# Strassen weights in a ring of their own, a fourth lo buffer, and the negated copy ahead of the hi cast, in a two-layer decoder trunk

## The chip, the cores and the metric

The kernel runs on one core of a Trainium2 chip. The metric is the device time of one execution in microseconds (us). Engines are TensorE (PE in the profile, its weight loads PEld), VectorE (DVE), ScalarE (ACT), GpSimd (POOL) and SyncE (SP, which here only issues DMAs). POOL issues a second, small kind of DMA. A change of about 0.2% is the least that a measurement of this kernel can tell.

## The reference

`x` is 256 tokens by 2048 channels; all arrays are fp32. Cut to what matters here:

```
mem_n = rms_norm(mem, mem_norm_g)
for l in range(2):
    hn = rms_norm(x, mix_norm_g[l])
    x = x + (even_mixer if l == 0 else odd_mixer)(hn, ...)   # matmuls with 2048-wide weights, attention or short conv
    x = x + cross_attention(rms_norm(x, xattn_norm_g[l]), mem_n, xq[l], xk[l], xv[l], xo[l])
    x = x + sq_relu_mlp(rms_norm(x, mlp_norm_g[l]), mlp_w1[l], mlp_w2[l])
return rms_norm(x, final_norm_g)

def sq_relu_mlp(h, w1, w2):                                  # 2048 -> 8192 -> 2048
    return square(relu(h @ w1)) @ w2
```

## The kernel before, in words

**Numbers in two parts.** Every weight and every activation is split into a hi part (a cast to the matmul's reduced fp32 type) and a lo part (the value minus hi). A product is hi weights times both parts of the activation (one 512-wide matmul per 128 × 128 block of weights) plus lo weights times hi activation (256 wide).

**Weights.** `weights()` brings 512 KB, half of a 2048 × 128 chunk, into a `raw` tile by a DMA that SP issues (L159). ACT casts it into `whi` (L160), DVE subtracts into `wlo` (L165). `raw` has a ring of 5 buffers, `whi` and `wlo` rings of 3 each; a tile that is to be written waits until the readers of the tile that held its buffer are done. With `added`, lo is made without DVE: ACT writes the negated raw into `wlo` (L162), and a DMA issued by POOL adds raw to the rounded negative in place (L163, the accumulate DMA).

**A chunk.** `proj_long` takes the two halves of a chunk and issues 15 hi matmuls, 16 lo matmuls (8 of each half), and the last hi matmul, which closes the sum.

**The MLP.** `mlp` works in four quarters of 2048 hidden channels per layer. In each quarter 16 chunks of w1 give the hidden activation: ACT and DVE add the two halves of the result (`sum`, L211, L212), DVE applies relu and the norm's factor (L833), ACT squares into `uu` (L835). After every fourth chunk `uu` is split into `hid` (L839, L840), and in the first three quarters DVE combines its token and channel halves (`combine`, L740 to L743) and splits that into `hs` (L745, L746).

In these three quarters of both layers, so six times, the product with w2 follows as eight Strassen steps (`for s in range(8)`). A step does half of its channels with seven products instead of eight: `seven_weights` loads two raw tiles of 512 KB (`raws`, L760, out of the ring of `raw`), makes `shi` and `slo` from the first (L767, L768; in the rings of `whi` and `wlo`), forms half-tile differences in place on DVE (L769, L771, L773, L774), splits the block b22 (L770, L772), and splits two tiles of combinations, t2 with t3 and then t1 with t4 (`tw`, ACT L776 and DVE L777). `seven_step` issues 21 matmuls into seven sums `p`, in the order b11, b21, t1, t4, b22, t3, t2. Then `proj_long` with `added` does an ordinary chunk of w2 (`mmn` in the profile), its second half by way of the accumulate DMA, and `residual` adds the result to `x` (L327). So a step uses three `wlo` buffers: `slo`, first half, second half. The weights of the first step are asked for after chunk 12 of the quarter's w1, those of the next ones at the head of each step; `seven_sum` (L798 to L803) ends the stretch.

**What sets the order.** The code only states what depends on what. A scheduler decides each engine's list from this, from the buffers that come free and from the order in the code; DVE's lo subtractions keep the code's order among themselves (`ordered`), and the matmuls do in stretches marked `strict`. Each engine then runs its own list in order.

Of the kernel before, what the change touches and what calls it, by code (L numbers as in the profile page):

```python
# [45 lines left out]
def trunk(ctx: ExitStack, tc: tile.TileContext, d):  # L46
    nc = tc.nc
    V, A, T, G = nc.vector, nc.scalar, nc.tensor, nc.gpsimd
# [1 line left out]
    const = ctx.enter_context(tc.tile_pool(name="const", bufs=1))  # L50
    xpool = ctx.enter_context(tc.tile_pool(name="xpool", bufs=1))
    half = ctx.enter_context(tc.tile_pool(name="half", bufs=13))
    wraw = ctx.enter_context(tc.tile_pool(name="wraw", bufs=5))
    wspl = ctx.enter_context(tc.tile_pool(name="wspl", bufs=3))
    tmp = ctx.enter_context(tc.tile_pool(name="tmp", bufs=2))
    small = ctx.enter_context(tc.tile_pool(name="small", bufs=4))
    pools = {}
    ps_mm = ctx.enter_context(tc.tile_pool(name="ps_mm", bufs=4, space=bass.MemoryType.PSUM))
    ps_at = ctx.enter_context(tc.tile_pool(name="ps_at", bufs=3, space=bass.MemoryType.PSUM))
    ps_nm = ctx.enter_context(tc.tile_pool(name="ps_nm", bufs=1, space=bass.MemoryType.PSUM))  # L60
# [5 lines left out]
    x = xpool.tile([P, NC, S], F32, name="x")  # L66
# [24 lines left out]
    def load_vec():  # L91
        nc.sync.dma_start(out=vec, in_=d["vec"][:, NG:])
        lv = vec[:, VEC["lam"] - NG:VEC["lam"] - NG + 256].rearrange("p (a b) -> p a b", a=4)
        lp = tmp.tile([P, S], F32, tag="t32", name="lp", bufs=7)[:, :128].rearrange("p (a b) -> p a b", a=2)
# [53 lines left out]
    def weights(src, added=False):  # L148

        run_later(rate[0], calls[0])  # L150
        run_stages(calls[0])
        calls[0] += 1
        raw = wraw.tile([P, 1024], F32, tag="raw", name="raw")
        hi = wspl.tile([P, 1024], F32R, tag="whi", name="whi")
        lo = wspl.tile([P, 1024], F32R, tag="wlo", name="wlo")
        n = 512 if calls[0] == 1 else 1024
        for i in range(0, 1024, n):
            o = slice(i, i + n)
            nc.sync.dma_start(out=raw[:, o], in_=src[:, o])  # L159
            A.copy(hi[:, o], raw[:, o])  # L160
            if added:
                A.activation(lo[:, o], raw[:, o], AF.Copy, scale=-1.0)  # L162
                G.dma_start(out=lo[:, o], in_=raw[:, o], accum_op=ALU.add)  # L163
            else:
                ordered(V.tensor_tensor(lo[:, o], raw[:, o], f(hi[:, o]), op=ALU.subtract), "lo")  # L165
        return hi, lo

# [104 lines left out]
    def spread(rows):  # L272
        ps = ps_nm.tile([P, 512], F32, tag="nm", name="nmb")[:, :S]
        for t in range(2):
            dg = tmp.tile([P, P], F32, tag="diag", name="diag")
            A.activation(dg, ident, AF.Copy, scale=rows[:, t:t + 1])
            mm(ps[:, t * P:(t + 1) * P], ones, dg, start=True, stop=True)
        return ps

    def rstd_rows(acc, n, pool=None, name="rrow"):  # L280

        v = small.tile([P, 2], F32, tag="rs_v", name="rs_v")
        V.tensor_scalar(v, mean_rows(acc, n), EPS, None, op0=ALU.add)
        return rsqrt(v, 2, pool, name)
# [12 lines left out]
        return y  # L297

    def to_sbuf(ps, pool=None, name="rb"):
        r = pool.tile([P, S], F32, tag=name, name=name) if pool else tmp.tile([P, S], F32, tag="rb", name=name, bufs=3)  # L300
        A.copy(r, ps)
        return r

# [3 lines left out]
    class SumSq:  # L307
# [4 lines left out]
        def add(self, src):  # L312
            if self.first:
                A.activation(self.acc, src, AF.Square)
                self.first = False
                return
            sq = tmp.tile([P, S], F32, tag="sq", name="sq")
            A.activation(sq, src, AF.Square)  # L318
            V.tensor_tensor(self.acc, self.acc, sq, op=ALU.add)  # L319

    def tmp32(name="t32"):
        return tmp.tile([P, S], F32, tag="t32", name=name, bufs=7)

    def residual(k, ps, nxt, ss, gname):

# [28 lines left out]
    def even_mixer():  # L354
        xa, ss = Act(NC, "xn"), SumSq()
# [30 lines left out]
        rc, r = rr["col"], rr["bc"]  # L386
# [62 lines left out]
        def heads_out(h, ahl):  # L449
            po = ps_at.tile([P, 512], F32, tag="at", name="po")[:, :S]  # L450
            hs = slice(h * P, (h + 1) * P)
            for kt in range(2):
                o = slice(kt * S, (kt + 1) * S)
                mm(po, vh[:, kt, hs], ahl[:, 0, o], start=kt == 0, stop=False)
                mm(po, vl[:, kt, hs], ahl[:, 0, o], start=False, stop=False)
                mm(po, vh[:, kt, hs], ahl[:, 1, o], start=False, stop=kt == 1)
            osq = tmp.tile([P, S], F32, tag="sq", name="osq")
# [297 lines left out]
    def seven_weights(src):  # L755


        raw = [wraw.tile([P, 4, 2, P], F32, tag="raw", name="raws") for _ in range(2)]
        for i, t in enumerate(raw):
            nc.sync.dma_start(out=t.rearrange("p c k f -> p c (k f)"),  # L760
                              in_=src[4 * i:4 * i + 4].rearrange("c p f -> p c f"))
# [5 lines left out]
        A.copy(sh, b1)  # L767
        V.tensor_tensor(sl, b1, f(sh), op=ALU.subtract)  # L768
# [4 lines left out]
        V.tensor_tensor(b2[:, 1], b2[:, 1], b1[:, 0], op=ALU.subtract)  # L773
        V.tensor_tensor(b1[:, 1], b2[:, 1], b1[:, 1], op=ALU.subtract)  # L774
        for t, b in ((t1, b1), (t2, b2)):
            A.copy(t[:, 0], b)  # L776
            V.tensor_tensor(t[:, 1], b, f(t[:, 0]), op=ALU.subtract)  # L777
# [45 lines left out]
    def mlp(l, xa, ss, gname):  # L823
        r = rstd(ss.acc, D)
        nxt = nss = None
        w1, w2 = d[f"w1{l}"], d[f"w2{l}"]
        uu = half.tile([P, 2, 2, 4, P], F32, tag="half", name="uu")
        for qd in range(4):
            hid = Act(NC, "hid")
            sa = SevenAct(hid) if qd < 3 else None  # L830
            for c in range(NC):
                u = summed(proj_long(w1[qd * NC + c], xa))
                V.scalar_tensor_tensor(u, u, 0.0, r, op0=ALU.max, op1=ALU.mult)  # L833
                v = uu[:, c // 4 % 2]
                A.activation(v[:, c % 4 // 2, c % 2 * 2:c % 2 * 2 + 2].rearrange("p h f -> p (h f)"), u, AF.Square)  # L835
                if c % 4 == 3:
                    t = hid.t[c // 4]
# [29 lines left out]
        return nxt, nss  # L867

    def scoped(name, fn, *a):
        with tc.tile_pool(name=name, bufs=4) as pools[name]:  # L870
            return fn(*a)

    def attentions(first):
        a = even_mixer() if first else odd_mixer(*state)
        return cross(0 if first else 1, *a)

    state = scoped("att", attentions, True)
    state = scoped("mlp", mlp, 0, *state, "mix1")
    state = scoped("att", attentions, False)
    _, ss = scoped("mlp", mlp, 1, *state, "final_norm_g")  # L880

    r = spread(rstd_rows(ss.acc, D))
    for g in range(8):
        o = slice(2 * g, 2 * g + 2)
        V.tensor_tensor(x[:, o], x[:, o], r.rearrange("p (a s) -> p a s", a=1).broadcast_to([P, 2, S]), op=ALU.mult)  # L885
        nc.sync.dma_start(out=d["yT"][:, o], in_=x[:, o])


# [58 lines left out]
```

## Time and profile before

| | before |
|---|---|
| median of 3 runs | 2995.7 us (2995.38 to 2997.54) |
| the profiled execution | 2999.52 us, of which the span is 2997.6 |
| mean granted clock of TensorE | 0.986 |
| busy: PE, DVE, ACT, POOL | 97%, 73%, 54%, 1% |
| instructions | 42425 |
| bytes moved by DMA | 565.16 MB, mean 189 GB/s |

In the profile a row of waits names the engine and line that waits, whom it waits for, the total in us, how often, and the longest. A row of the timeline has the start, the duration, the engine and line, the operation with out<-in, and in brackets the idle time of the engine just before it and what ended that. A row of groups has the total busy time and the mean in ns, then the idle time ahead of the group's instructions. A row of windows has a stretch and its length, the busy times (and instruction counts) of PE, PEld, DVE, ACT and POOL, the granted clock, the DMA engines' busy share and GB/s.

### The profile page before, as it was taken

What the parts mean: (1) busy time and instruction counts of PE and PEld (TensorE: products, weight loads), DVE (VectorE), ACT (ScalarE), POOL (GpSimd) and SP (SyncE); (2) the same over time, 40 slices, a digit from 0 to 9 for tenths busy, and PEclk for the clock granted to TensorE, in tenths of its full rate; (3) what the DMA queues carried; (4) which work ended last, traced back from release to release, by engine and by line L of the source; (5) the groups of instructions that cost most, each with busy time, mean ns of one, the idle gap of its engine ahead of it and who ended that gap; (6) DMA issues with size and microseconds to landing.
All of it is one profiled execution on the core that took longest, in us unless ns stands there. A gap on an engine that the chain in (4) does not pass through costs nothing. (4 is left out here: it accounts for less than half of the span.)

```text
span 2997.6 us, 42425 instructions
## 1 busy us (share of the span) xinstructions
PE 2902.7 (97%) x16072; PEld 2529.8 (84%) x16072; DVE 2201.0 (73%) x3414; ACT 1605.3 (54%) x2275; POOL 44.7 (1%) x68
## 2 busy tenths in 40 slices
PE   9999999999999899999999999999999999999998
PEld 7888888888878778888888888888888787887887
DVE  7899987766777777766677765477767767777665
ACT  6666455555554555545444444455555545555553
POOL 0000000000000000000000000000000000000000
PEclk9999999999999999999999999999999999999999
DMA  7464665445576675766556656654455766757664
GB/s 248 160 200 159 194 190 189 156 155 183 179 208 201 181 218 175 211 201 190 183 193 202 197 195 191 193 187 159 154 181 180 205 202 184 224 182 206 199 187 139
DMA packets 194171, 565.16 MB, mean 189 GB/s; under 512 B 17456, under 2 KB 66736, under 8 KB 193968
## 3 DMA queue, kind: packets, MB, share of 16 engines
q1 hardware_dynamic: 187056, 537.30, 55.8%
q0 software_dynamic: 6912, 25.17, 4.3%
q8 instruction: 126, 2.06, 0.3%
q14 instruction: 77, 0.63, 0.1%
HBM read 535.13 MB, written 2.10 MB: 179 GB/s over the span
## 5 line engine op out<-in xcount | busy, mean ns | idle before, releaser
L165 DVE TENSOR_TENSOR wlo<-raw,whi 128x1024 fp32r<-128x1024 f32 (+1 forms) x865 | 1056.7, 1222 | 471.0 <-PE mm L139 187.2
L160 ACT CAST whi<-raw 128x1024 fp32r<-128x1024 f32 (+1 forms) x913 | 958.4, 1050 | 590.1 <-PE mm L139 271.8
L139 PE MATMUL mm<-xn,whi 128*128 128x512 f32 x3840 | 945.7, 394 | 0.0
L139 PEld LDWEIGHTS mm<-xn,whi 128*128 128x128 f32 x3840 | 708.3, 190 | 135.2
L139 PEld LDWEIGHTS mm<-xn,wlo 128*128 128x128 f32 x3840 | 507.5, 194 | 49.3 <-DVE wlo L165 25.9
L139 PE MATMUL mm<-xn,wlo 128*128 128x256 f32 x3840 | 516.8, 285 | 23.4 <-DVE wlo L165 23.4
L211 ACT COPY sum<-mm 128x256 f32<-128x256 f32 x272 | 101.1, 372 | 580.2 <-PE mm L139 580.0
L212 DVE TENSOR_TENSOR sum<-mm,sum 128x256 f32<-128x256 f32 x272 | 115.1, 423 | 105.7 <-ACT sum L211 105.3
L139 PE MATMUL mmn<-hid,whi 128*128 128x512 f32 x768 | 191.9, 392 | 0.0
L139 PEld LDWEIGHTS mmn<-hid,whi 128*128 128x128 f32 x768 | 145.5, 189 | 28.0
L139 PE MATMUL mmn<-hid,wlo 128*128 128x256 f32 x768 | 111.7, 293 | 48.5 <-DMA wlo<-raw 48.4
L139 PEld LDWEIGHTS mmn<-hid,wlo 128*128 128x128 f32 x768 | 103.4, 196 | 58.8 <-DMA wlo<-raw 55.0
L777 DVE TENSOR_TENSOR tw<-raws,tw 128x1024 fp32r<-128x1024 f32 x96 | 114.7, 1221 | 34.6 <-ACT tw L776 34.6
L139 PE MATMUL mmr<-whi,mem 128*128 128x512 f32 x512 | 137.3, 390 | 0.0
L139 PE MATMUL mm<-mem,whi 128*128 128x512 f32 x512 | 126.3, 393 | 0.0
L139 PE MATMUL mm<-o,whi 128*128 128x512 f32 x512 | 124.7, 392 | 0.0
L139 PE MATMUL mm<-hid,whi 128*128 128x512 f32 x512 | 122.7, 391 | 0.0
L139 PE MATMUL p<-tw,hs 128*128 128x512 f32 x432 | 116.6, 394 | 3.2 <-DVE tw L777 3.0
L511 DVE SCALAR_TENSOR_TENSOR cv<-a,vec,cv 128x255 f32<-128x255 f32 (+14 forms) x240 | 111.8, 466 | 2.9
L139 PEld LDWEIGHTS mmr<-whi,mem 128*128 128x128 f32 x512 | 95.8, 188 | 19.6
L139 PEld LDWEIGHTS mm<-hid,whi 128*128 128x128 f32 x512 | 94.1, 188 | 18.6 <-DVE hid L840 0.5
L139 PEld LDWEIGHTS mm<-o,whi 128*128 128x128 f32 x512 | 93.7, 188 | 18.6 <-DVE o L254 0.9
(208 smaller groups left out, 3284.3 us busy)
## 6 DMA issues: line engine op xcount, KB each, us to landing
raw<-w SPq DMA_DIRECT2D x416, 512.0 KB, 4.2
raws<-w SPq DMA_DIRECT2D x96, 512.0 KB, 3.9
raw<-odd_in SPq DMA_DIRECT2D x96, 512.0 KB, 4.6
raw<-even_in SPq DMA_DIRECT2D x64, 512.0 KB, 4.2
raw<-xk SPq DMA_DIRECT2D x64, 512.0 KB, 3.6
raw<-xv SPq DMA_DIRECT2D x64, 512.0 KB, 3.6
raw<-xq SPq DMA_DIRECT2D x64, 512.0 KB, 4.0
raw<-xo SPq DMA_DIRECT2D x64, 512.0 KB, 3.8
```

Source lines behind the costliest of these rows:

```text
L139: i = T.matmul(*a, **k)
L160: A.copy(hi[:, o], raw[:, o])
L165: ordered(V.tensor_tensor(lo[:, o], raw[:, o], f(hi[:, o]), op=ALU.subtract), "lo")
L211: A.copy(t, ps[:, S:])
L212: V.tensor_tensor(t, ps[:, :S], t, op=ALU.add)
L511: ordered(V.scalar_tensor_tensor(cv[:, c, s:], a[:, c, :S - s], col("conv_a_w", i + j), cv[:, c, s:], op0=ALU.mult, op1=ALU.add), "lo")
L777: V.tensor_tensor(t[:, 1], b, f(t[:, 0]), op=ALU.subtract)
```

## The change

- `raws` leave the ring of `raw`, which has 4 buffers instead of 5, for a ring of 4 of their own in the MLP's pool. `uu` leaves its tile of the pool `half` and takes tiles of that ring, one per four chunks.
- `wlo` has 4 buffers instead of 3. The tile with t1 and t4 moves into the place that `uu` left in `half`.
- With `added`, the negated copy and the accumulate DMA stand ahead of the hi cast.
- The small tiles `t32`, `rb`, `sq` and `diag` get their buffer counts by stage: 7, 3, 2, 2 as before in the mixers and cross-attention, 3, 1, 1, 1 in the MLP. The final norm moves into the MLP's stage (`last`).

```diff
-    wraw = ctx.enter_context(tc.tile_pool(name="wraw", bufs=5))
+    wraw = ctx.enter_context(tc.tile_pool(name="wraw", bufs=4))
...
+    BUFS = {"att": {"t32": 7, "rb": 3, "sq": 2, "diag": 2}, "mlp": {"t32": 3, "rb": 1, "sq": 1, "diag": 1}}
+
+    def scratch(tag, name, shape=(P, S)):
+        return pools[pools["now"]].tile(list(shape), F32, tag=tag, name=name, bufs=BUFS[pools["now"]][tag])
...
-        lo = wspl.tile([P, 1024], F32R, tag="wlo", name="wlo")
+        lo = wspl.tile([P, 1024], F32R, tag="wlo", name="wlo", bufs=4)
...
             nc.sync.dma_start(out=raw[:, o], in_=src[:, o])
-            A.copy(hi[:, o], raw[:, o])
             if added:
                 A.activation(lo[:, o], raw[:, o], AF.Copy, scale=-1.0)
                 G.dma_start(out=lo[:, o], in_=raw[:, o], accum_op=ALU.add)
-            else:
+            A.copy(hi[:, o], raw[:, o])
+            if not added:
                 ordered(V.tensor_tensor(lo[:, o], raw[:, o], f(hi[:, o]), op=ALU.subtract), "lo")
...
-        raw = [wraw.tile([P, 4, 2, P], F32, tag="raw", name="raws") for _ in range(2)]
+        raw = [pools["mlp"].tile([P, 4, 2, P], F32, tag="raws", name="raws", bufs=4) for _ in range(2)]
...
-        sl = wspl.tile([P, 2, 4, P], F32R, tag="wlo", name="slo")
+        sl = wspl.tile([P, 2, 4, P], F32R, tag="wlo", name="slo", bufs=4)
...
-        t1, t2 = [pools["mlp"].tile([P, 2, 2, 4, P], F32R, tag=f"tw{i}", name="tw", bufs=1) for i in range(2)]
+        t1 = half.tile([P, 2, 2, 4, P], F32R, tag="half", name="tw")
+        t2 = pools["mlp"].tile([P, 2, 2, 4, P], F32R, name="tw", bufs=1)
...
-        uu = half.tile([P, 2, 2, 4, P], F32, tag="half", name="uu")
...
-                v = uu[:, c // 4 % 2]
+                if c % 4 == 0:
+                    v = pools["mlp"].tile([P, 2, 4, P], F32, tag="raws", name="uu", bufs=4)
...
     def scoped(name, fn, *a):
+        pools["now"] = name
```

In the changed kernel the lines are numbered a little higher: the sum is L215, the negated copy L165, the accumulate DMA L166, the hi cast L167, the lo subtraction L169, `hs` L749 and L750, `shi` L772, `tw` L781 and L782, the square L840. The lists differ in many rows, since the scheduler makes them anew; the number of instructions on each engine is the same but for waits. Three places follow. In the rows, "waits" names the engines and DMA queues whose signal the instruction needs.

**First place: ACT in chunks 11 to 14 of a quarter, where the first step's weights are prepared.** `sum` is a chunk's result, `whi` an ordinary hi cast, `shi`, `b` and `tw` belong to the Strassen weights. Before, from chunk 11's sum on:

```order
L211 COPY sum<-mm 128x256 [waits PE_49]
L767 CAST shi<-raws 128x1024 [waits DMAHW5_49,Activation_49]
L835 ACTIVATE uu<-sum 128x256 [waits DVE_49]
L839 CAST hid<-uu 128x4x256 [waits Activation_49]
L160 CAST whi<-raw 128x1024 [waits DMAHW7_49,PE_49]
L211 COPY sum<-mm 128x256 [waits PE_49]
L160 CAST whi<-raw 128x1024 [waits DMAHW0_49]
L776 CAST tw<-raws 128x1024 [waits DVE_49]
L745 CAST hs<-uu 128x8x128 [waits DVE_49]
L835 ACTIVATE uu<-sum 128x256
L776 CAST tw<-raws 128x1024 [waits DVE_49]
L160 CAST whi<-raw 128x1024 [waits DVE_49,DMAHW1_49,PE_49,Activation_49]
```

After, from chunk 12's sum on:

```order
L215 COPY sum<-mm 128x256 [waits PE_49]
L749 CAST hs<-uu 128x8x128 [waits DVE_49]
L840 ACTIVATE uu<-sum 128x256 [waits DVE_49]
L772 CAST shi<-raws 128x1024 [waits DMAHW1_49]
L167 CAST whi<-raw 128x1024 [waits DMAHW5_49]
L775 CAST b_8436<-raws 128x512 [waits DMAHW2_49]
L167 CAST whi<-raw 128x1024 [waits DMAHW6_49]
L167 CAST whi<-raw 128x1024 [waits DMAHW7_49,DVE_49,PE_49]
L781 CAST tw<-raws 128x1024 [waits DVE_49] x2
L215 COPY sum<-mm 128x256 [waits PE_49]
L167 CAST whi<-raw 128x1024 [waits DMAHW0_49,Activation_49]
```

Before, the first hi cast of chunk 13 stands ahead of chunk 12's sum (the second `sum` row); after, it stands behind that sum, the `hs` cast, the square and the `shi` cast, and a group of casts stands together ahead of the next sum.

SP's list at the same place has the loads. Before:

```order
L159 DMA raw<-w 128x1024 [waits DMAHW7_49,DVE_49]
L760 DMA raws<-w 128x4x256 [waits DMAHW0_49,DVE_49,Activation_49]
L760 DMA raws<-w 128x4x256 [waits DMAHW1_49,DVE_49]
L159 DMA raw<-w 128x1024 [waits DMAHW2_49,DVE_49]
L159 DMA raw<-w 128x1024 [waits DMAHW3_49,DVE_49]
L159 DMA raw<-w 128x1024 [waits DMAHW4_49,DVE_49]
L159 DMA raw<-w 128x1024 [waits DMAHW6_49,DVE_49]
```

After:

```order
L163 DMA raw<-w 128x1024 [waits DMAHW4_49,DVE_49]
L764 DMA raws<-w 128x4x256 [waits PE_49,Pool_49]
L764 DMA raws<-w 128x4x256
L764 DMA raws<-w 128x4x256 [waits DVE_49]
L163 DMA raw<-w 128x1024 [waits DMAHW5_49,DVE_49]
L163 DMA raw<-w 128x1024 [waits DMAHW6_49,DVE_49]
L163 DMA raw<-w 128x1024 [waits DMAHW7_49,DVE_49]
```

Before, two raw tiles of the Strassen weights are loaded between ordinary ones; after, three of them in a row, the third already the second step's, ahead of the loads that follow.

**Second place: ACT in a Strassen step in the middle of a stretch.** Before, from the hi cast of the accumulated half on:

```order
L160 CAST whi<-raw 128x1024 [waits DMAHW6_49,PE_49,Activation_49]
L162 ACTIVATE wlo<-raw 128x1024 [waits DMASW3_49]
L767 CAST shi<-raws 128x1024 [waits DMAHW7_49,PE_49,Activation_49]
L770 CAST b_9048<-raws 128x512 [waits DMAHW0_49,PE_49,Activation_49]
L160 CAST whi<-raw 128x1024 [waits DVE_49,DMAHW1_49,PE_49,Activation_49]
L776 CAST tw<-raws 128x1024 [waits DVE_49,Activation_49]
L776 CAST tw<-raws 128x1024 [waits Activation_49]
```

After, the same step:

```order
L165 ACTIVATE wlo<-raw 128x1024 [waits DMAHW6_49,DMASW0_49,PE_49]
L167 CAST whi<-raw 128x1024 [waits PE_49,Activation_49]
L772 CAST shi<-raws 128x1024 [waits DMAHW7_49,PE_49,Activation_49]
L775 CAST b_9051<-raws 128x512 [waits DMAHW0_49,PE_49,Activation_49]
L781 CAST tw<-raws 128x1024 [waits DVE_49,PE_49,Activation_49]
L781 CAST tw<-raws 128x1024 [waits DVE_49]
L167 CAST whi<-raw 128x1024 [waits DMAHW1_49,PE_49,Activation_49]
```

The negated copy (`wlo`) and the hi cast behind it have changed places; the first half's `whi` has moved from between `b` and `tw` to the end of the step.

**Third place: DVE at the end of the first Strassen step of a quarter.** The first `tw` row is t2's lo part, the second t1's; `x` is the residual's add. Before:

```order
L743 TENSOR_TENSOR uu<-uu 128x2x128 [waits DVE_49]
L777 TENSOR_TENSOR tw<-raws,tw 128x1024 [waits PE_49,Activation_49]
L327 TENSOR_TENSOR x<-x,mmn 128x256 [waits PE_49]
L777 TENSOR_TENSOR tw<-raws,tw 128x1024 [waits Activation_49]
L746 TENSOR_TENSOR hs<-uu,hs 128x8x128 [waits Activation_49]
L327 TENSOR_TENSOR x<-x,mmn 128x256 [waits DVE_49]
L165 TENSOR_TENSOR wlo<-raw,whi 128x1024 [waits DMAHW1_49]
```

After:

```order
L747 TENSOR_TENSOR uu<-uu 128x2x128 [waits DVE_49]
L782 TENSOR_TENSOR tw<-raws,tw 128x1024 [waits PE_49,Activation_49]
L169 TENSOR_TENSOR wlo<-raw,whi 128x1024 [waits DMAHW2_49]
L750 TENSOR_TENSOR hs<-uu,hs 128x8x128 [waits Activation_49]
L331 TENSOR_TENSOR x<-x,mmn 128x256 [waits PE_49]
L782 TENSOR_TENSOR tw<-raws,tw 128x1024 [waits Activation_49]
L331 TENSOR_TENSOR x<-x,mmn 128x256 [waits DVE_49]
```

The lo subtraction (`wlo`) and the `hs` subtraction, which stood behind t1's `tw`, now stand ahead of it.

More of the change, by code (lines that the diff above doesn't have):

```diff
@@ L93, in load_vec @@
         lv = vec[:, VEC["lam"] - NG:VEC["lam"] - NG + 256].rearrange("p (a b) -> p a b", a=4)
-        lp = tmp.tile([P, S], F32, tag="t32", name="lp", bufs=7)[:, :128].rearrange("p (a b) -> p a b", a=2)
+        lp = scratch("t32", "lp")[:, :128].rearrange("p (a b) -> p a b", a=2)
         V.tensor_tensor(lp, lv[:, 0:4:2], lv[:, 1:4:2], op=ALU.mult)
@@ L274, in spread @@
         for t in range(2):
-            dg = tmp.tile([P, P], F32, tag="diag", name="diag")
+            dg = scratch("diag", "diag", (P, P))
             A.activation(dg, ident, AF.Copy, scale=rows[:, t:t + 1])
@@ L299, in to_sbuf @@
     def to_sbuf(ps, pool=None, name="rb"):
-        r = pool.tile([P, S], F32, tag=name, name=name) if pool else tmp.tile([P, S], F32, tag="rb", name=name, bufs=3)
+        r = pool.tile([P, S], F32, tag=name, name=name) if pool else scratch("rb", name)
         A.copy(r, ps)
@@ L316, in add @@
                 return
-            sq = tmp.tile([P, S], F32, tag="sq", name="sq")
+            sq = scratch("sq", "sq")
             A.activation(sq, src, AF.Square)
@@ L321, in tmp32 @@
     def tmp32(name="t32"):
-        return tmp.tile([P, S], F32, tag="t32", name=name, bufs=7)
+        return scratch("t32", name)
     def residual(k, ps, nxt, ss, gname):
@@ L456, in heads_out @@
                 mm(po, vh[:, kt, hs], ahl[:, 1, o], start=False, stop=kt == 1)
-            osq = tmp.tile([P, S], F32, tag="sq", name="osq")
+            osq = scratch("sq", "osq")
             A.activation(osq, po, AF.Square)
@@ L875, in attentions, with last @@
         return cross(0 if first else 1, *a)
+    def last(*a):
+        _, ss = mlp(1, *a)
+        r = spread(rstd_rows(ss.acc, D))
+        for g in range(8):
+            o = slice(2 * g, 2 * g + 2)
+            V.tensor_tensor(x[:, o], x[:, o], r.rearrange("p (a s) -> p a s", a=1).broadcast_to([P, 2, S]), op=ALU.mult)
+            nc.sync.dma_start(out=d["yT"][:, o], in_=x[:, o])
     state = scoped("att", attentions, True)
@@ L879, in trunk @@
     state = scoped("att", attentions, False)
[L880 to L886, printed above, removed]
+    scoped("mlp", last, *state, "final_norm_g")
 def _cols(v):
```

## The prediction

> **What bounds the kernel now.** I read the busy shares first, then TensorE's waits, then the stretches in which the waits lie, one stretch as a timeline, and last the groups of instructions for prices.
>
> ```profile
> PE 2902.7 (97%) x16072; PEld 2529.8 (84%) x16072; DVE 2201.0 (73%) x3414; ACT 1605.3 (54%) x2275; POOL 44.7 (1%) x68
> ...
> PE mmn L139 <- DMA wlo<-raw: 48.4, 30, 3.7
> PE mm L139 <- DVE wlo L165: 23.4, 6, 3.9
> ...
> PE p L139 <- DVE tw L777: 3.0, 7, 0.7
> ```
>
> TensorE (PE) is busy nearly throughout, so only its waits and its clock can be won; matmuls are neither added nor removed. Its two large waits both lie at the Strassen steps: for the accumulate DMA that completes `wlo` (48.4 us), and six times, once ahead of each Strassen stretch, for a lo subtraction (23.4 us). The six stretches, of which the first and the last row stand with the sum:
>
> ```profile
> core 0: us, PE busy (x) PEld busy (x) DVE busy (x) ACT busy (x) POOL busy (x), PEclk, DMA share, GB/s
> 827.30:922.21 94.91, 85.98 (x425) 72.35 (x424) 73.14 (x97) 53.57 (x58) 6.94 (x8) 0.98 0.73 207
> ...
> 2705.03:2801.77 96.74, 87.95 (x426) 73.31 (x424) 73.34 (x97) 53.38 (x58) 6.79 (x8) 0.96 0.72 202
> sum 572.76, PE 521.02 PEld 438.16 DVE 439.19 ACT 321.01 POOL 40.87; mean PE 86.84 PEld 73.03 DVE 73.20 ACT 53.50 POOL 6.81
> ```
>
> The first step of a stretch meets no such wait, and shows what a step costs when all is there:
>
> ```profile
> 827.30 0.62 PE L139 MATMUL p<-shi,hid 128*128 128x512 f32 x2
> ...
> 832.09 3.56 PE L139 MATMUL mmn<-hid,whi 128*128 128x512 f32 x15
> ...
> 837.63 0.62 PE L139 MATMUL p<-shi,hid 128*128 128x512 f32 x2
> ```
>
> From 827.30 to 837.63 are 10.33 us; 48 such steps are 495.8. The stretches last 572.8, so 77.0 us lie in waits and in half-clock spells behind them. That is the most the steps can give. The last step of the stretch shows the chain:
>
> ```profile
> 907.61 1.21 PE L139 MATMUL mmn<-hid,wlo 128*128 128x256 f32 x8 [1.42 <-DMA wlo<-raw]
> 908.66 0.40 PE L139 MATMUL mmn<-hid,whi 128*128 128x512 f32 x1
> 909.13 1.05 ACT L160 CAST whi<-raw 128x1024 fp32r<-128x1024 f32 x1 [0.73 <-PE mmn L139]
> 910.09 1.06 ACT L162 ACTIVATE wlo<-raw 128x1024 fp32r<-128x1024 f32 x1
> 911.44 0.85 POOL L163 DMA_DIRECT2D wlo<-raw  x1 [11.15 <-ACT wlo L162]
> 920.92 1.22 PE L139 MATMUL mmn<-hid,wlo 128*128 128x256 f32 x8 [2.73 <-DMA wlo<-raw]
> ...
> DMA to landing us min/median/max: 5.2/7.4/9.7
> ```
>
> The hi cast waits for the last hi matmul to free its buffer, the negated copy follows it, then the DMA. From second lo half to DMA are 3.83 us (907.61 to 911.44), plus a median landing of 7.4: 11.2, over 10.33, so each step waits for the one before.
>
> **Term A, the steps.** A negated copy made ahead of the cast need only have its `wlo` buffer. With four of these and three used per step (slo, first half, second half), the buffer is the one of the previous step's first half. Its eight matmuls end some 9.3 us into that step (in the clean step: 15 hi matmuls from 4.79 to 8.2, eight lo matmuls of 1.1). Copy to DMA take 1.35 (910.09 to 911.44): issued at 10.65, and wanted by the next step's second lo half at 10.33 + 9.2 = 19.5. A landing of up to 8.8 is therefore free; 7.4 is below it. The 5.2 and the 9.7 are the bounds: nothing, or 0.9 in each of 42 steps (38 us). If one in ten of the 42 lands as late as 9.7, that is 4 × 0.9 = 3.6 us, which I take since the median is clear of the limit.
>
> What is late next is the second step's t1. Its lo part is DVE's last product of the weights:
>
> ```profile
> 840.01 0.50 PE L139 MATMUL p<-tw,hs 128*128 128x512 f32 x1 [0.39 <-DVE tw L777]
> ...
> L746 DVE TENSOR_TENSOR hs<-uu,hs 128x1024 fp32r<-128x1024 f32 x24 | 29.3, 1222 | 10.8 <-ACT hs L745 10.8
> L777 DVE TENSOR_TENSOR tw<-raws,tw 128x1024 fp32r<-128x1024 f32 x96 | 114.7, 1221 | 34.6 <-ACT tw L776 34.6
> L165 DVE TENSOR_TENSOR wlo<-raw,whi 128x1024 fp32r<-128x1024 f32 (+1 forms) x865 | 1056.7, 1222 | 471.0 <-PE mm L139 187.2
> ```
>
> Before, it came 12.71 us after the stretch began, with t1 due at 10.33 + 1.38 (828.68, the end of the six matmuls ahead in the first step) = 11.71. In the new order on DVE one lo subtraction and the hs subtraction, 1.22 us each, stand ahead of it: 15.15 if nothing else moves, 12.71 if idle DVE time takes both. I take 14.1, as about 1 us of DVE's waits in that stretch fills: 2.4 us late, six times, 14.4 us. The wait also costs clock:
>
> ```profile
> 850.09 1.60 PE L139 MATMUL mmn<-hid,wlo 128*128 128x256 f32 x8 [2.49 <-DMA wlo<-raw]
> ...
> 850.70:854.12 3.42, 3.42 (x13) 2.84 (x12) 1.89 (x3) 1.99 (x2) 0.84 (x1) 0.50 0.81 262
> 907.61:911.00 3.39, 3.39 (x19) 2.98 (x20) 3.39 (x4) 2.65 (x3) 0.00 (x0) 1.00 0.60 173
> 922.38:925.80 3.42, 3.42 (x9) 2.65 (x9) 3.09 (x5) 1.14 (x2) 0.00 (x0) 0.50 0.98 317
> ```
>
> After a wait of 2.49 the granted clock is 0.50 for 3.4 us (1.7 us lost); after 1.42 it stays 1.00; after 2.73 (at 920.92) it is 0.50 again. So 2.4 us lie between; I count two in three, 6 × 1.7 × 0.65 = 6.6 us. [...]
>
> A: 495.8 + 3.6 + 14.4 + 6.6 = 520.4, against 572.8: −52.4 us.
>
> **Term B, the lead-in.** The first step's weights are prepared while PE does the last w1 chunks. Before:
>
> ```profile
> 804.67 3.81 PE L139 MATMUL mm<-xn,whi 128*128 128x512 f32 x16
> ...
> 812.39 3.21 PE L139 MATMUL mm<-xn,wlo 128*128 128x256 f32 x16 [3.90 <-DVE wlo L165]
> ```
>
> After, on ACT, chunk 13's first hi cast no longer precedes chunk 12's sum; it stands behind that sum, an hs cast, a square into `uu` and the shi cast. The square's `uu` shares four buffers with the raw tiles, three of which SP loads ahead, so it takes the one that the hs subtraction on DVE frees. Prices:
>
> ```profile
> L211 ACT COPY sum<-mm 128x256 f32<-128x256 f32 x272 | 101.1, 372 | 580.2 <-PE mm L139 580.0
> L745 ACT CAST hs<-uu 128x1024 fp32r<-128x1024 f32 x24 | 25.1, 1046 | 0.0
> L835 ACT ACTIVATE uu<-sum 128x256 f32<-128x256 f32 x128 | 53.6, 419 | 5.9 <-DVE sum L833 5.6
> L767 ACT CAST shi<-raws 128x1024 fp32r<-128x1024 f32 x48 | 50.3, 1048 | 16.0 <-DMA raws<-w 13.5 <-PE p L139 2.4
> L160 ACT CAST whi<-raw 128x1024 fp32r<-128x1024 f32 (+1 forms) x913 | 958.4, 1050 | 590.1 <-PE mm L139 271.8 <-PE mmn L139 119.8 <-PE mmr L139 96.6
> ```
>
> From the end of chunk 12, PE waits 0.37 + 1.05 + 1.22 (hs subtraction) + 0.42 + 1.05 + 1.05 = 5.2 us for chunk 13. If the square need not wait for DVE it is 3.9, and if the scheduler's lists overlap as before, no more than the old 3.9. Chunk 14's first cast stands behind both tw casts and chunk 13's sum, about 1.7 us more (0 to 3). I take 5.2 + 1.7 − 3.9 = 3.0 per quarter, 18 us, bounds 0 and 6 × 4.3 = 26. Clock: the new second wait closes the clock about once more (2 us); the spells that follow a stretch's last accumulate wait, as at 922.38, go in three quarters (−5). B: +15.
>
> **Term C, the other edits.** The ring of raw weights shrinks to four everywhere. In a mixer:
>
> ```profile
> L159 SPq DMA_DIRECT2D raw<-w x18: 327/328/328, 1390.0 to 1437.8; - x18
> ...
> DMA to landing us min/median/max: 3.4/3.7/4.8
> ```
>
> A half comes every 2.8 us (47.8 / 17), so four buffers turn in 11.2 us; landing, cast and subtraction use 3.7 + 1.05 + 1.22 = 6.0. PE's weights stay ahead; 0 to 6 us, taken 1. Single `diag`, `sq` and `rb` buffers make the pairs of a norm serial, a cast of 0.4 and two matmuls a few times: 1 us. Moving `tw` to another pool and the final norm into a function issue the same instructions: nothing, as the same engines do them at the same place.
>
> Sum: −52.4 + 15 + 2 = −35.4 against the profiled 2999.5: 2964. That execution lies 3.8 us above the median of the runs, so **2960**.
>
> **The rivals.** (1) Slower: the accumulate lands later. SP's loads for the next step no longer stand behind its landing:
>
> ```profile
> SPq L760 <- DMA wlo<-raw: 251.2, 36, 9.1
> ```
>
> These 251 us of holding back kept loads out of the accumulate's way; the same bytes now also come in 10.4 us per step, not 11.9, a DMA share of 0.84 for 0.73. Each us of landing beyond 8.8 costs 42 us, with clock 48. From a median of 9.7, today's maximum, the kernel is slower than before by a measurable amount; at 9.8 it takes 3008. For it: the spread 5.2 to 9.7 is already that of loads in the way. Against it: half the landings stay at 7.4 at a share of 0.73, though many loads run beside them. [...]
>
> (2) DVE becomes the bound. Per step it has slo, five half products, two tw and one lo subtraction and two adds into x:
>
> ```profile
> L768 DVE TENSOR_TENSOR slo<-raws,shi 128x1024 fp32r<-128x1024 f32 x48 | 58.8, 1225 | 44.9 <-ACT shi L767 44.4
> L773 DVE TENSOR_TENSOR raws<-raws 128x512 f32<-128x512 f32 x48 | 33.1, 690 | 1.2
> L327 DVE TENSOR_TENSOR x<-x,mmn 128x256 f32<-128x256 f32 x96 | 39.9, 416 | 29.3 <-PE mmn L139 29.3
> ```
>
> 1.22 + 5 × 0.69 + 2 × 1.22 + 1.22 + 2 × 0.42 = 9.17 us; with today's waits for ACT (44.9 / 48 and 34.6 / 48) 10.8, 0.5 above the clean step: 42 × 0.5 = 21 us, and 2981, or 2990 where the copy made early delays ACT's casts by a further 0.2. Against it: with the new order DVE finds lo subtractions and adds to do in those waits.
>
> (3) The lead-in is starved: SP issues three raw loads (1.5 MB) ahead of chunk 13's raw. At the 317 GB/s of the row at 922.38 each is 1.65 us, so up to 5.0 × 6 = 30 us: 2990. Against: they are issued chunks earlier.
>
> (4) The lead-in costs nothing new, since lists overlap: −15, 2945, or 2940 without the second step's clock losses.
>
> (5) The change does not do what it says: SP loads the accumulated raw too late for an early copy, the step stays at 11.2 plus its waits, and B alone is left: 3011 at worst, 2996 if the lead-in is unchanged.
>
> **How the numbers follow.** Chances: forecast (2945 to 2978) 0.57; (4) 0.12; (2) 0.12, (3) 0.09, both 2980 to 2996; (1) 0.06; (5) 0.04. A change under 0.2% (6 us) cannot be told from none here: faster is below 2989.7, slower above 3001.7. Faster: 0.57 + 0.12 + about half of (2) and (3) = 0.81; same: the other half and a little of (5), 0.10; slower: 0.09. The range 2938 to 2990 leaves out (1), (5) and the upper part of (2) and (3).
>
> **What would show it.** Right: the wait of `mmn` for the accumulate falls from 48.4 to under 8; the stretches sum to about 520; a wait of `p` for tw of 2 to 2.5 us, six times; the wait of `mm` ahead of a stretch rises to 5 and moves to the hi cast; landings stay near 7.4. Wrong: landings of 9 and more with the `mmn` wait still there (1); waits of `p` in every step (2); `mm` waits beyond 7 us or for the raw's DMA (3).

## The result and the profile after

The changed kernel takes 2950.9 us (median of 4 runs, 2948.9 to 2951.9) against 2995.5 before: a ratio of 0.9851, 95% interval 0.9834 to 0.9868, or 44.6 us less. The forecast was 2960, with a range of 2938 to 2990.

The page's busy times and the waits of TensorE in the profile after:

```profile
PE 2884.1 (98%) x16072; PEld 2514.7 (85%) x16072; DVE 2205.1 (75%) x3414; ACT 1607.4 (54%) x2275; POOL 44.7 (2%) x68
...
PE mm L143 <- ACT whi L167: 22.3, 6, 3.7
PE mmn L143 <- DMA wlo<-raw: 11.8, 12, 1.9
PE p L143 <- DVE tw L782: 11.6, 6, 1.9
...
PE nmb L143 <- ACT diag L280: 3.3, 2, 2.9
```

The wait for the accumulate has gone from 48.4 us to 11.8. The wait for t1's `tw` is new (3.0 to 11.6, six times 1.94). The wait ahead of each stretch is still there, 22.3 for 23.4, but is now for the hi cast. The six stretches (windows, the sum) and the accumulate's landing:

```profile
sum 529.11, PE 505.58 PEld 429.02 DVE 444.45 ACT 315.43 POOL 40.87; mean PE 84.26 PEld 71.50 DVE 74.08 ACT 52.57 POOL 6.81
...
DMA to landing us min/median/max: 5.4/8.1/10.8
```

572.8 us have become 529.1, which is 43.7 of the 47.6 between the two profiled executions (2999.52 and 2951.88). By the starts of the steps in the two traces, 28 of the 48 steps now last exactly the 10.33 us of a clean step; before, 8 did. One chain, of the accumulate that the third step needs (timeline):

```profile
848.81 2.08 PE L143 MATMUL mmn<-hid,wlo 128*128 128x256 f32 x16
...
849.96 1.06 ACT L165 ACTIVATE wlo<-raw 128x1024 fp32r<-128x1024 f32 x1 [0.38 <-PE mmn L143]
850.72 0.40 PE L143 MATMUL mmn<-hid,whi 128*128 128x512 f32 x1
...
851.21 1.05 ACT L167 CAST whi<-raw 128x1024 fp32r<-128x1024 f32 x1 [0.19 <-PE mmn L143]
...
851.32 0.84 POOL L166 DMA_DIRECT2D wlo<-raw  x1 [9.75 <-ACT wlo L165]
...
862.11 1.21 PE L143 MATMUL mmn<-hid,wlo 128*128 128x256 f32 x8 [1.86 <-DMA wlo<-raw]
```

The negated copy starts as soon as the first eight lo matmuls are through (849.96), ahead of the last hi matmul and of the hi cast that waits for it. The DMA goes out 2.51 us after the first lo matmul (851.32 − 848.81); before, it went out 3.83 us after the start of the second eight, so only once the accumulate before had landed. This accumulate took 10.7 us to land, the second longest of all, and still cost PE only 1.86.

### The profile page after: what moved, and what is told of

Its sections match the earlier page's. It is cut to its first block, busy times and chain, and to the rows that moved or that the text cites. A ratio compares the mean times of both kernels' runs of the same rounds, so it can differ in the third digit from the quotient of the medians.

```text
span 2950.1 us, 42343 instructions
## 1 busy us (share of the span) xinstructions
PE 2884.1 (98%) x16072; PEld 2514.7 (85%) x16072; DVE 2205.1 (75%) x3414; ACT 1607.4 (54%) x2275; POOL 44.7 (2%) x68
## 4 chain that ended last, share of the span: by engine, by line
PE 55%; DMA 5%; issue 3%; DVE 2%; ACT 1%; DVEq 0%; POOLq 0%; POOL 0%; ACTq 0%; SPq 0%
PE mm L143 45%; DMA wlo<-raw 3%; PE mmr L143 3%; PE mmn L143 3%; PE p L143 3%; DMA raw<-w 2%; ACT whi L167 0%; DVE wlo L169 0%; PE pox L143 0%; PE sx L143 0%; ACT shi L772 0%; DVE tw L782 0%; DVE slo L773 0%; ACT tw L781 0%; DVE raws L774 0%
## 5 line engine op out<-in xcount | busy, mean ns | idle before, releaser
L167 ACT CAST whi<-raw 128x1024 fp32r<-128x1024 f32 (+1 forms) x913 | 958.1, 1050 | 504.0 <-PE mm L143 276.9
L169 DVE TENSOR_TENSOR wlo<-raw,whi 128x1024 fp32r<-128x1024 f32 (+1 forms) x865 | 1056.0, 1221 | 162.5 <-ACT whi L167 150.3
L143 PE MATMUL mm<-xn,whi 128*128 128x512 f32 x3840 | 951.2, 396 | 22.4 <-ACT whi L167 22.3
L143 PEld LDWEIGHTS mm<-xn,wlo 128*128 128x128 f32 x3840 | 500.7, 191 | 23.9
L143 PE MATMUL mm<-xn,wlo 128*128 128x256 f32 x3840 | 508.4, 282 | 0.0
L215 ACT COPY sum<-mm 128x256 f32<-128x256 f32 x272 | 101.0, 371 | 544.3 <-PE mm L143 533.2
L331 DVE TENSOR_TENSOR x<-x,mm 128x256 f32<-128x256 f32 x192 | 80.7, 420 | 124.9 <-PE mm L143 121.3
L781 ACT CAST tw<-raws 128x1024 fp32r<-128x1024 f32 x96 | 97.2, 1048 | 84.3 <-DVE raws L778 76.5
L143 PE MATMUL p<-tw,hs 128*128 128x512 f32 x432 | 117.3, 396 | 11.6 <-DVE tw L782 11.6
L782 DVE TENSOR_TENSOR tw<-raws,tw 128x1024 fp32r<-128x1024 f32 x96 | 114.2, 1221 | 17.1 <-ACT tw L781 17.1
L143 PEld LDWEIGHTS mmn<-hid,wlo 128*128 128x128 f32 x768 | 99.3, 191 | 18.3 <-DMA wlo<-raw 14.5
L143 PE MATMUL mmn<-hid,wlo 128*128 128x256 f32 x768 | 103.1, 285 | 11.9 <-DMA wlo<-raw 11.8
```

The costliest lines, as they stand in the source:

```text
L143: i = T.matmul(*a, **k)
L215: A.copy(t, ps[:, S:])
L331: V.tensor_tensor(x[:, k], x[:, k], ps[:, i * S:(i + 1) * S], op=ALU.add)
```

## The experiments

The theory at first: an early copy needs its buffer and its place ahead of the cast. The rivals: one of the two is enough, the ring of the raws carries the gain, or the landing grows and takes it back.

**The fourth buffer.** 

```diff
-        lo = wspl.tile([P, 1024], F32R, tag="wlo", name="wlo", bufs=4)
+        lo = wspl.tile([P, 1024], F32R, tag="wlo", name="wlo")
...
-        sl = wspl.tile([P, 2, 4, P], F32R, tag="wlo", name="slo", bufs=4)
+        sl = wspl.tile([P, 2, 4, P], F32R, tag="wlo", name="slo")
```

> The changed kernel with three wlo buffers again; the negated copy stays ahead of the hi cast in the code. Theory: the fourth buffer carries the gain. With three, wlo of the accumulated half takes the buffer of the previous step's accumulated half, free only at that step's end, and ACT's list has the hi cast ahead of the copy again; the chain of 3.83 us plus landing closes once per step, the six stretches take 560 to 575 us, mmn waits 35 us or more, in all 2980 to 2997. Rival: the place of the copy in the code carries it; then 2951 to 2965.

2990.6 us, 0.9965 of before (0.9952 to 0.9979). The sum of the stretches, and PE's wait, in its profile:

```profile
sum 562.92, PE 513.39 PEld 431.06 DVE 439.60 ACT 318.54 POOL 40.87; mean PE 85.56 PEld 71.84 DVE 73.27 ACT 53.09 POOL 6.81
...
PE mmn L143 <- DMA wlo<-raw: 40.0, 30, 2.7
...
854.28 1.06 ACT L167 CAST whi<-raw 128x1024 fp32r<-128x1024 f32 x1 [3.00 <-issue]
855.24 1.06 ACT L165 ACTIVATE wlo<-raw 128x1024 fp32r<-128x1024 f32 x1
```

Without the buffer most of the wait is back (40.0 of 48.4). The code still asks for the copy first, but on ACT the hi cast stands ahead of it again (855.24 behind 854.28).

**The place of the copy.**

```diff
             nc.sync.dma_start(out=raw[:, o], in_=src[:, o])
+            A.copy(hi[:, o], raw[:, o])
             if added:
                 A.activation(lo[:, o], raw[:, o], AF.Copy, scale=-1.0)
                 G.dma_start(out=lo[:, o], in_=raw[:, o], accum_op=ALU.add)
-            A.copy(hi[:, o], raw[:, o])
-            if not added:
+            else:
```

> The changed kernel with the hi cast ahead of the negated copy in the code again; four wlo buffers stay. Theory: the scheduler places the copy by when its buffer comes free, so with four buffers it stands ahead of the cast whatever the code's order: stretches 525 to 535, 2945 to 2957. Rival, the reading of the prediction (the copy stands behind a cast that waits for the last hi matmul): stretches 565 to 575, 2985 to 2997.

2952.2 us, 0.9836 (0.982 to 0.9851): no difference from the changed kernel. The rows of ACT at the same step, where the cast stands first in the code:

```profile
850.21 1.06 ACT L166 ACTIVATE wlo<-raw 128x1024 fp32r<-128x1024 f32 x1 [0.39 <-PE mmn L143]
851.46 1.05 ACT L164 CAST whi<-raw 128x1024 fp32r<-128x1024 f32 x1 [0.18 <-PE mmn L143]
...
sum 528.79, PE 503.96 PEld 427.00 DVE 444.54 ACT 315.46 POOL 40.87; mean PE 83.99 PEld 71.17 DVE 74.09 ACT 52.58 POOL 6.81
```

Both lists fit a scheduler that puts first what can start first: with four buffers that is the copy, with three it is the cast, whatever the code's order.

**The ring of the raws.**

```diff
-        raw = wraw.tile([P, 1024], F32, tag="raw", name="raw")
+        raw = pools[pools["now"]].tile([P, 1024], F32, tag="raw", name="raw", bufs={"att": 4, "mlp": 5}[pools["now"]])
...
-        raw = [pools["mlp"].tile([P, 4, 2, P], F32, tag="raws", name="raws", bufs=4) for _ in range(2)]
+        raw = [pools["mlp"].tile([P, 4, 2, P], F32, tag="raw", name="raws", bufs=5) for _ in range(2)]
...
-                    v = pools["mlp"].tile([P, 2, 4, P], F32, tag="raws", name="uu", bufs=4)
+                    v = pools["mlp"].tile([P, 2, 4, P], F32, tag="uu", name="uu", bufs=2)
```

> The changed kernel with the Strassen raws back in one ring of five with raw during the MLP (that ring then lives in the stage's pool, four buffers in the mixers), and uu in two buffers of its own. Theory A: the raws' own ring matters, since SP otherwise holds a step's loads until the accumulate before has landed; t1 and shi come late, stretches 545 to 565, 2965 to 2990. Theory B: the loads that are held back shorten the landing (median back from 8.1 to 7.4), and the stretches fall to 515 to 525, 2937 to 2947.

3003.8 us, 1.002 (1.0007 to 1.0033), outside the ranges of both theories. Against the changed kernel some 24 us of this lie outside the stretches: here the ring starts anew with each stage, and at three changes of stage SP waits 15 to 19 us for a norm (`accsq`), which is probably the reason. So only the stretches are compared. Their sum, PE's wait, SP's, and the landing:

```profile
sum 556.20, PE 510.99 PEld 430.72 DVE 444.32 ACT 315.44 POOL 40.86; mean PE 85.16 PEld 71.79 DVE 74.05 ACT 52.57 POOL 6.81
...
PE mmn L142 <- DMA wlo<-raw: 32.3, 25, 2.7
...
SPq L763 <- DMA wlo<-raw: 267.2, 36, 10.4
SPq L162 <- DVE accsq L322: 98.1, 19, 18.6
...
DMA to landing us min/median/max: 5.3/9.1/11.5
```

Theory B falls, and with it the reason of the prediction's rival (1): holding the next step's Strassen loads behind the accumulate (267.2 us, as the 251.2 before) did not make it land sooner, its median is 9.1 for 8.1. By the issue times of the two traces, 2.15 loads are issued in the two us ahead of an accumulate here, and 1.33 in the changed kernel: what is held back here comes in a burst, just as the next accumulate goes out. The 21 accumulates with three loads issued in these two us took 10.2 us on average, the 14 with one took 6.1. Theory A has the size of the stretches right (556 in 545 to 565) but for another reason: `mmn` waits, not t1. The longer landing is only a part of that. undo_swap has the same median (9.05) with waits of 13.0 us. Beside it, 22 of the 36 accumulates for the steps three to eight go out late here, 0.2 to 3.8 us later than 2.51 us after the first lo matmul; in the changed kernel and in undo_swap none does. How the 27 us divide between the two, no run here separates.

**The fourth buffer without the ring.**

```diff
-    wraw = ctx.enter_context(tc.tile_pool(name="wraw", bufs=5))
+    wraw = ctx.enter_context(tc.tile_pool(name="wraw", bufs=4))
...
-        lo = wspl.tile([P, 1024], F32R, tag="wlo", name="wlo")
+        lo = wspl.tile([P, 1024], F32R, tag="wlo", name="wlo", bufs=4)
...
-        sl = wspl.tile([P, 2, 4, P], F32R, tag="wlo", name="slo")
+        sl = wspl.tile([P, 2, 4, P], F32R, tag="wlo", name="slo", bufs=4)
```

> The kernel before with only the fourth wlo buffer, paid for by a ring of four raw buffers that the Strassen raws still share (five do not fit beside it). Theory: the buffer alone is not enough, since a step's raws wait on SP for the accumulate before to land and a late t1 or shi takes the place of the late accumulate: stretches 560 to 585, 2985 to 3010. Rival: the buffer alone carries the gain: stretches 525 to 540, 2950 to 2965.

3005.3 us, 1.0027 (1.0017 to 1.0037): slower than before. The stretches, and what ACT waits for in this kernel:

```profile
sum 581.23, PE 522.26 PEld 435.86 DVE 437.78 ACT 316.62 POOL 40.87; mean PE 87.04 PEld 72.64 DVE 72.96 ACT 52.77 POOL 6.81
...
ACT wlo L162 <- DMA raw<-w: 42.3, 28, 3.7
ACT b L770 <- DMA raws<-w: 35.5, 36, 2.4
...
ACT shi L767 <- DMA raws<-w: 21.9, 26, 1.6
```

The buffer is free, but the raw that is to be copied into it has not come (42.3 us): a step has four raw tiles of both kinds, and with four buffers none is left to load ahead. So the stretches read: before 572.8; own ring with three lo buffers 562.9; four lo buffers in a shared ring of five 556.2, of four 581.2; both 529.1. The two parts need each other.

**The loads beside the accumulate.** Steps two to eight get no raws of their own, so their products lack their weights:

```diff
-        raw = [pools["mlp"].tile(...) for _ in range(2)]
-        for i, t in enumerate(raw):
+        if s < 1:
+            kept[s] = [pools["mlp"].tile(...) for _ in range(2)]
+        raw = kept[0]
+        for i, t in enumerate(raw if s < 1 else ()):
             nc.sync.dma_start(...)
```

> The changed kernel in which steps two to eight of each quarter reuse the raw tiles of the first instead of loading their own (so these products are left without their weights); casts, products and the accumulate stay. Half the bytes of a step go. Theory: the landing of the accumulate is set by the loads beside it; median 6 to 7 instead of 8.1, none above 8.8, mmn waits under 1 us in all instead of 11.8, stretches 510 to 516 (eight clean steps of 10.33 and the one wait for t1), lead-in unchanged or 1 us shorter: 2928 to 2937. Rival: the landing is long for another reason (POOL's queue, the tile's place), stays near 8.1: 2945 to 2953.

2936.2 us, 0.9793 (0.9778 to 0.9808). Its waits, sum and landing:

```profile
PE mm L143 <- ACT whi L167: 22.3, 6, 3.7
PE p L143 <- DVE tw L786: 11.7, 6, 1.9
...
sum 510.75, PE 499.10 PEld 426.04 DVE 443.09 ACT 315.15 POOL 40.86; mean PE 83.18 PEld 71.01 DVE 73.85 ACT 52.52 POOL 6.81
...
DMA to landing us min/median/max: 5.2/7.4/8.5
```

No landing is above 8.5, and no step waits for an accumulate; all 42 steps other than the second of each quarter last 10.33. The median of 7.4 is above the 6 to 7 expected. It is the tail that cost time, up to 10.8 us with the loads and 8.5 without them, and here the loads make the tail. That no landing of up to 8.5 costs anything also fits the limit of 8.8.

**The lead-in.**

```diff
-                if c == 12 and sa:
+                if c == 10 and sa:
```

> The changed kernel with the first Strassen step's weights asked for after chunk 10 instead of chunk 12 of the quarter. Theory: the wait of 3.72 us ahead of each stretch comes from casts that fall together with the split of uu after chunk 11; moved off it, the six waits (22.3 us) and the half-clock spells behind them (some 8 us) go: 2915 to 2928. Rival: the same casts make the same wait two chunks earlier: 2945 to 2957.

2920.9 us, 0.9731 (0.971 to 0.9752). Its waits of PE and its stretches:

```profile
PE mmn L143 <- DMA wlo<-raw: 13.8, 15, 1.4
PE p L143 <- DVE tw L782: 11.8, 6, 2.1
...
sum 530.62, PE 504.89 PEld 427.92 DVE 444.47 ACT 315.99 POOL 40.95; mean PE 84.15 PEld 71.32 DVE 74.08 ACT 52.67 POOL 6.82
```

The wait of `mm` is gone altogether, and the 16 chunks between two stretches take 89.07 us (16 × 5.57 = 89.1) instead of 94.7 to 95.9. The stretches are as they were.

**The wait for t1, and an earlier accumulate.** Three edits, the first two on prepare_at_10:

```diff
# late_combine
-                    if sa:
+                    if sa and c < 15:
                         sa.combine(c // 4, v)
...
                         b = seven_weights(w2[:NS, :, o:o + 2 * P])
+                    if s == 1:
+                        sa.combine(3, v)
```

```diff
# added_half_first, in proj_long
-        (h0, l0), (h1, l1) = [weights(src[:, g * 1024:(g + 1) * 1024], added and g == 1) for g in range(2)]
+        halves = [weights(src[:, g * 1024:(g + 1) * 1024], added and g == 1) for g in ((1, 0) if added else (0, 1))]
+        (h0, l0), (h1, l1) = halves[::-1] if added else halves
```

> prepare_at_10, and the combination of the last four chunks' uu and its split into hs (needed only by the seventh step) moved behind the second step's weights. Theory: the wait of 1.94 for t1 in the second step is DVE's queue; with 2.9 us of work moved off it goes (p waits 11.8 to under 2), but the hs cast then stands on ACT near the negated copy and the accumulate waits grow by up to 4 us per quarter: 2910 to 2935. Rival: the t1 wait is bound by ACT's casts and stays, no change: 2917 to 2925.

> prepare_at_10, with the accumulated half asked for ahead of the plain half in each step, so its wlo takes the buffer of the previous slo, free 1.4 us into that step instead of 9.3. Theory: the accumulate goes out some 5 us earlier and no longer waits (mmn waits 13.8 to under 2), while the casts moved ahead push t1 later (p waits from 11.8 to 25 to 40): 2912 to 2935. Rival: the landing grows as it meets other loads, mmn waits stay above 8: 2925 to 2945.

> added_half_first and late_combine together. Theory: added_half_first left only the second step long (13.5 to 16.3 us), since the cast of t1 stands on ACT behind the first half's hi cast and the hs cast; with the hs cast moved back the wait of p falls from 15.3 us to under 8, accumulates stay on time (mmn wait under 2): stretches 510 to 520, 2893 to 2906. Rival: the work moved back makes t1 late in the third and fourth steps instead (up to 2.9 us each): 2905 to 2925.

late_combine 2909.5 us (0.9706, 0.9691 to 0.972), added_half_first 2907.2 (0.9695, 0.9679 to 0.9711), both together 2891.8 (0.9636, 0.9622 to 0.9651). A line of PE's waits of the first, two of the second, two and the sum of the third:

```profile
PE mmn L143 <- DMA wlo<-raw: 18.9, 17, 2.4
```

```profile
PE p L143 <- ACT tw L782: 9.9, 6, 1.7
...
PE p L143 <- DVE tw L783: 5.4, 6, 0.9
```

```profile
PE p L143 <- ACT tw L782: 2.5, 2, 1.6
PE p L143 <- DVE tw L783: 2.1, 3, 0.7
...
sum 504.17, PE 499.33 PEld 426.04 DVE 447.51 ACT 313.61 POOL 35.66; mean PE 83.22 PEld 71.01 DVE 74.58 ACT 52.27 POOL 5.94
```

late_combine has no wait of `p` left, so the t1 wait was DVE's queue, and the accumulate's rises to 18.9, as expected. added_half_first has no wait for the accumulate, and t1 waits more (15.3), less than the 25 expected. Together they leave 4.6 us of waits, and 504.2 us in the stretches against 495.8 for clean steps; the rival came in part, since what is left lies in the third steps. All three kernels are faster than the low end of their ranges (2910, 2912, 2893). The last is the fastest version.

A third move, the products in the order b11, b21, b22, t3, t2, t1, t4, gained nothing:

> both_moves with the products in the order b11, b21, b22, t3, t2, t1, t4, so that t1 is wanted 2.1 us later in a step. Theory: what is left of the wait for t1 goes, the wait for t3 (made first) is at most 1 us per quarter: 2890 to 2903. Rival: t3 and t2 are now the late ones, and t1's tile, freed later, delays the next cast: 2903 to 2920.

> late_combine with the products in the order b11, b21, b22, t3, t2, t1, t4; the accumulated half stays second. Theory: late_combine has lost the wait for t1 already, so the order of the products gains nothing and the accumulate waits (18.9 us) stay: 2905 to 2917. Rival: the second step still runs late by the work moved back, and gives 1 us per quarter: 2898 to 2905.

On both_moves it gives 2894.8 us (0.9647, 0.9631 to 0.9663), stretches 511.1, with the third step of each quarter at 12.4 to 14.5 us; on late_combine 2913.3 (0.9708, 0.9694 to 0.9722), stretches 523.9 for 520.7. The first time lies in its theory's range, but not by its mechanism: the waits of `p` did not go (6.6 us for 4.6). The median is 3 us above that of both_moves, less than a measurement can tell; the stretches are 6.9 us longer, by third steps that run late, as the rival says. In the second the order gains nothing, as its theory says, but the waits behind that changed:

```profile
PE mmn L143 <- DMA wlo<-raw: 10.8, 11, 1.9
PE p L143 <- DVE tw L782: 7.5, 12, 1.0
```

The accumulate's wait, which was to stay at 18.9, fell to 10.8, and waits of `p` took its place.

## Why the prediction was right, and where its terms were off

**Term A, the steps: −52.4 forecast, −43.7 measured.** The mechanism held: the copy starts 9.3 us into a step, and an accumulate may take 8.8 us to land. Nine steps of the changed kernel wait behind a clean step, and each waits for what its accumulate's landing exceeds 8.88 us (9.04: 0.15; 10.31: 1.43); few_raws, whose longest is 8.5, has no wait. Two sizes were off. The late landings were put at 3.6 us. The excess of the stretches over clean steps is 33.3 us (529.1 − 495.8), of which the second steps' share is 16.6 (six of them 2.23 us over a clean one, two with 1.62 more from half clock), so late landings, with the half clock behind one of them, cost 16.7. The step that failed was taking the landings from before as they were; in shorter steps, with the Strassen loads free, their median rose from 7.4 to 8.1 and their maximum from 9.7 to 10.8.

The t1 term with its clock was 21.0 in the forecast and 16.6 in the trace. The time at which t1's lo part comes was nearly right, 14.26 us after the stretch began for 14.1; what was wrong is when it is due:

```profile
841.06 1.22 DVE L782 TENSOR_TENSOR tw<-raws,tw 128x1024 fp32r<-128x1024 f32 x1
842.33 0.50 PE L143 MATMUL p<-tw,hs 128*128 128x512 f32 x1 [1.94 <-DVE tw L782]
```

Two matmuls on t1's hi part go ahead of the one that needs the lo part, so that one is due 1.99 us into the step (842.33 − 1.94 − 838.40), at 12.32 and not at 11.71, and the wait is 1.94 us and not 2.4. The prediction's own row of 840.01 says so, with a wait of 0.39 where a due time of 11.71 would make it 1.0.

**Rival (1), the landing that grows.** It named the growth, but neither its reason nor its price held. The reason was that loads no longer stand behind the accumulate. The Strassen loads do not, but SP, whose list runs in order, still stands behind the accumulates as long as before, now with the ordinary loads (before, then after):

```profile
SPq L159 <- DMA wlo<-raw: 94.9, 12, 9.2
```

```profile
SPq L163 <- DMA wlo<-raw: 352.2, 48, 10.5
```

With the 251.2 of the Strassen loads that was 346.1 us before. The price of 42 us for each us beyond 8.8 holds where a late accumulate follows a clean step. Behind a step that has itself waited for one, the next has that much more room: 9.68 us behind a step 1.16 too long cost nothing. So undo_swap, with a median of 9.05, has stretches of 528.8 us, no longer than the changed kernel's 529.1. The rival's DMA share of 0.84 goes with steps of 10.4 us; by the prediction's own sum they are 10.8 (520.4 / 48), and the share measured is 0.76 to 0.80. How far loads can lengthen a landing, no run here bounds: one trace, t1_last, has landings of 4.5 and of 11.7 us.

**The place of the copy in the code did nothing.** The prediction put the gain down to a copy ahead of the cast with a free buffer, without saying which of the two edits makes it so. undo_swap and undo_lo4 show that of these two it is the buffer alone: with it, the copy goes ahead of the cast in either order of the code. The order of two lines in the code is only a wish to a scheduler, and the list that it made of undo_swap could have shown this without a run.

**The raws' own ring was not given a price.** It stood in the prediction only as a danger. raws_shared puts it at 27 us of the stretches (556.2 − 529.1), and lo4_alone shows the buffer worthless without room for the raws.

**Term B, the lead-in: +15 forecast.** With C (+2) it makes +17 for all outside the stretches; measured are −3.9 (47.6 − 43.7 in the two profiled executions). The chain on ACT (timeline after):

```profile
805.91 0.37 ACT L215 COPY sum<-mm 128x256 f32<-128x256 f32 x1 [2.74 <-PE mm L143]
806.30 1.04 ACT L749 CAST hs<-uu 128x1024 fp32r<-128x1024 f32 x1
...
807.25 0.41 ACT L840 ACTIVATE uu<-sum 128x256 f32<-128x256 f32 x1
807.38 1.23 DVE L750 TENSOR_TENSOR hs<-uu,hs 128x1024 fp32r<-128x1024 f32 x1 [0.18 <-ACT hs L749]
807.57 1.03 ACT L772 CAST shi<-raws 128x1024 fp32r<-128x1024 f32 x1
808.50 1.04 ACT L167 CAST whi<-raw 128x1024 fp32r<-128x1024 f32 x1
...
809.60 5.30 PE L143 MATMUL mm<-xn,whi 128*128 128x512 f32 x15 [3.72 <-ACT whi L167]
```

The order was as foretold, but the square (807.25) did not wait for the hs subtraction (807.38): the step that failed is the buffer that `uu` was said to take. The row of SP that waits shows who took it, a load of raws:

```profile
SPq L764 <- DVE hs L750: 49.6, 6, 8.3
```

So the wait is 3.72, near the lower figure of 3.9 that the prediction had given for this case, and the second wait of 1.7 in chunk 14 did not come. The half-clock spells right after a stretch are gone as forecast; before, they were two whole ones (from 922.38 and 2420.83, granted clock 0.50) and a part of a third (from 1304.67), worth some 4 us by an estimate (half of 3.4 us for a whole one) for the 5 forecast. The two errors, 8.7 us too much gain in A and 21 too much loss in B and C, have opposite signs; left over are 12 us against the profiled execution and 9 against the median. So that the forecast came so near is in part luck. Of its own signs only the wait for t1, six times, came close to its size (1.94 us for 2 to 2.5); the wait for the accumulate fell to 11.8 and not under 8, the wait ahead of a stretch moved to the hi cast but did not rise, and the landings grew.

**Rivals (2), (3) and (5)** did not come about: DVE's work per step fits into the 10.33 us of the clean steps, chunk 13 has no wait for a raw's DMA, and the step no longer waits for the one before it. Of (4) the first part came, that the lead-in costs nothing new.

**The clock.** The same wait of 1.94 us for t1 was followed by full clock in one quarter (after 842.33) and by half clock in another (after 2311.30):

```profile
842.40:845.80 3.40, 3.40 (x15) 2.83 (x16) 3.33 (x5) 0.62 (x1) 0.00 (x0) 1.00 0.93 242
2312.20:2315.60 3.40, 3.40 (x10) 2.62 (x9) 2.80 (x5) 0.62 (x1) 0.00 (x0) 0.50 1.03 233
```

Two of six fell to 0.50 (from 2312.19 and from 2680.83), where two in three were assumed for a longer wait. What decides which of these equal waits is followed by half clock, the traces here do not show.

## What to carry to other kernels

A chain that closes once per step is opened by the buffer that lets its first link start early; ask which buffer a late instruction takes and when its last reader is done, and then whether what fills it can come as early. Where a scheduler orders the engines, price the lists that it makes, not the order of the lines: a swap of two lines did nothing here, and moving one call by two chunks or a side job by one step gave some 30 and 11 us. Loads that a full ring held back did not by that leave the way free to others: in raws_shared they came later, in a burst (2.15 loads for 1.33 in the two us ahead of an accumulate), and the accumulate's median landing was 9.1 us for 8.1.

## What the runs showed of the hardware

In these runs the landing of the 512 KB accumulate DMA went with the loads that were issued just ahead of it. Over the 13 traces, 428 accumulates with no load or one load issued in the two us before took 7.1 us on average, 126 with two took 8.7, and 70 with three or four took 10.0; the ranges overlap, and the extremes are 4.5 and 11.7 us for the same bytes. Before the change no accumulate had three, and the 16 with two took 7.8 for 7.3 of the other 32; in the changed kernel 29 with none or one took 7.4, 11 with two 9.2, and the 8 with three or four 10.0. The number of loads under way or issued during the landing told less, since a longer landing meets more loads: in the changed kernel 16 accumulates with two took 6.95 us and 27 with four took 9.0, but before, 2 with two took 7.9 and 16 with four took 7.6. What it is in these loads that lengthens a landing, no run here separates.
